# Where the weights of the values products and of attention's sums lie beside their moving data in SBUF

## The chip, the cores and the metric

The kernel runs on one core of a Trainium2 chip. The metric is the device time of one execution in microseconds (us), taken as the median of several runs. Every matmul here reads two operands from SBUF: 128 columns of weights, which are loaded into TensorE first, and the moving data, which are then streamed through it. The trace has a record for each of the two (PEld for the load, PE for the matmul), and it names the clock that TensorE was granted.

## The reference

Two groups of tokens (`x_prompt` and `x_sample`, each 512 x 1024 in float32) pass through the same trunk of two layers, and a final RMS norm closes it. Cut to what matters:

```python
def trunk(x, ...):
    # layer 0: differential attention, 8 heads, V is 512 x 2048
    h = rms_norm(x, norm_g[0], eps)
    q, k, v, gate = split(h @ da_w_in)            # da_w_in: 1024 x 8192
    q, k = rotary_half(q) * d ** -0.5, rotary_half(k)
    p = softmax(q @ k.T)                          # two maps per head
    a = p[:, :, 0] - lam * p[:, :, 1]
    o = rms_norm(a @ v, subln_g) * (1 - lambda_init) * silu(gate)
    x = x + o @ da_w_out                          # 2048 x 1024
    # layer 1: bidirectional retention, 8 heads, V is 512 x 2048
    h = rms_norm(x, norm_g[1], eps)
    q, k, v, gate = split(h @ ret_w_in)           # ret_w_in: 1024 x 6144
    o = retention(q, k, v, decay_fwd) + flipped retention(q, k, v, decay_bwd)
    o = rms_norm(o, subln_g) * silu(gate)
    x = x + o @ ret_w_out                         # 2048 x 1024
    return rms_norm(x, final_norm_g, eps)
```

## The kernel before

**Numbers in two parts.** All matmuls take `float32r` operands. To keep accuracy, each operand is split into a high and a low part (`hi_of` on ScalarE, `lo_of` on VectorE), and each product is the sum of three passes: high by high, high by low, low by high (`PASSES`).

**Four stages.** The input projection of layer 0 runs from about 40 to 640 us, attention with its output projection to about 1120 us, the input projection of layer 1 to about 1495 us, and retention with its output projection to the end. The input projections use a seven-product scheme in place of eight products per 2 x 2 block (`Unit`, products P1 to P7). The right operands of a projection, the `B` tiles made from the normed input, lie in `slot`s; the left ones are weights from HBM, combined on VectorE and split into the ring `ws` of seven buffers.

**Which operand is loaded and which moves.** In a "pair" unit (queries, keys, gates) the `ws` tile is loaded as TensorE's weights and a `B` tile of 512 columns moves (line 616). In a "wide" unit (the values V, eight units, four in each layer) it is the other way round: 128 columns of a `B` tile are loaded, and 256 columns of the `ws` tile move (line 626). One product of a wide unit is 4 token blocks x 4 parts of K x 3 passes = 48 matmuls, so the eight units have 8 x 7 x 48 = 2688. In attention, `av` (line 1198) forms the sum of values over keys: 128 columns of `vt` (V) are loaded, 256 columns of the transposed attention map `aT` move; 24 matmuls each for 32 pairs of token blocks, 768 in all. Retention has four kinds of 256-column matmuls: scores (line 1332, keys loaded, queries move), states (line 1356, `kt` loaded, V moves), the near part (line 1376, V loaded, scores move) and the far part (line 1384, state loaded, queries move). The output projections (line 908) load `oT` and move a `ws` tile of 512 columns; twelve of them, at the very end, move 256.

**Where the tiles lie.** The slots that matter lie in one tile called `arena`, 1024 words (4096 bytes) apart; `slot(..., shift)` moves a tile by so many words inside it. The other slots are tiles of 4096 bytes and begin at the same address modulo 256 as the arena (128). The seven `ws` buffers are separate tiles behind the arena, with small tiles (`pad`) between them, into which the kernel puts its small columns (norm sums, maxima, constants of up to 32 words). Every step from one 128-column or 256-column block to the next within a tile is a multiple of 256 bytes. So for each kind of matmul one number says how its two operands lie to each other: the distance from the start of the moving data to the start of the weights, modulo 256 bytes. "Distance" means this below. Before the change it follows from the shifts:

| matmuls | line | moving columns | count | weights at (bytes) | moving at (bytes) | distance |
|---|---|---|---|---|---|---|
| pair units | 616 | 512 | 3360 | 0 (`ws`) | 0 (`B`) | 0 |
| attention scores | 1133 | 512 | 384 | 0 | 0 | 0 |
| output projections | 908 | 512 (12 have 256) | 1542 | 0 | 0 | 0 |
| values products | 626 | 256 | 2688 | 0 (`B`) | -64 (`ws`) | 64 |
| attention's sums | 1198 | 256 | 768 | 64 (`vt`) | 0 (`aT`) | 64 |
| retention: scores | 1332 | 256 | 192 | 128 | 64 | 64 |
| retention: states | 1356 | 256 | 192 | 64 | 0 | 64 |
| retention: near part | 1376 | 256 | 384 | 0 | 64 | 192 |
| retention: far part | 1384 | 256 | 192 | 0 | 64 | 192 |

(Addresses are counted from the start of the arena, modulo 256.) Where one kind follows another, the next one's weights are loaded beside the last one's moving data, and the distance is that of these two: from a state (line 1356) to a score (line 1332) it is 128 - 0 = 128.

**Order of the work.** The whole program is recorded as a list of operations (`plan.op`) with modelled costs, then `Plan.arrange` orders it for each engine by those costs and by due times. Addresses have no part in the costs. SyncE's queue issues the DMAs.

Of the kernel before, what the change touches and what calls it, by code (L numbers as in the profile page):

```python
# [9 lines left out]
F32 = mybir.dt.float32  # L10
F32R = mybir.dt.float32r
# [4 lines left out]
P = 128  # L16
# [237 lines left out]
def trunk_kernel(  # L254
# [13 lines left out]
    ar = ctx.enter_context(tc.tile_pool(name="ar", bufs=1))  # L268
# [10 lines left out]
    def view(pool, tag, i, size, shape, dt=F32):  # L279


        n = math.prod(shape[1:])
        if (tag, i) not in places:
            if size <= 32 and pool in (cp, wk):
                k = next(k for k, used in enumerate(gaps) if used + size <= PAD - 16)
                places[tag, i] = pads[k][:, gaps[k]:gaps[k] + size]
                gaps[k] += size
            else:
                places[tag, i] = pool.tile([P, size], F32, tag=f"{tag}{i}", name=f"{tag}_{i}", bufs=1)
        t = places[tag, i][0:shape[0], 0:n]  # L290
        if dt != F32:
            t = t.bitcast(dt)
        if len(shape) == 3:
            t = t.rearrange("p (a b) -> p a b", a=shape[1])
        elif len(shape) == 4:
            t = t.rearrange("p (a b c) -> p a b c", a=shape[1], b=shape[2])
        return t

    def work(tag, shape, bufs, dt=F32, name=None):
        size = SIZE.get(tag, shape[1])  # L300
        return Buf(plan, tag, bufs, lambda i: view(wk, tag, i, size, shape, dt))

    PAD = 64
    gaps = [0] * (WS_BUFS - 1)
    arena = ar.tile([P, 18 * 1024 + 112], F32R, tag="arena", name="arena")
    rings, pads = [], []
    for i in range(WS_BUFS):
        rings.append(ar.tile([P, 1024 + 16], F32R, tag=f"ws{i}", name=f"ws_{i}"))
        if i < WS_BUFS - 1:
            pads.append(ar.tile([P, PAD - 16], F32, tag=f"pad{i}", name=f"pad_{i}"))  # L310

    def slot(n, shape, dt=F32R, shift=0):

        size = math.prod(shape[1:])
        at = None if n in (12, 13) or n >= 20 else n if n < 12 else n - 2
        if at is None:
            assert not shift
            cnt[0] += 1  # L320
            label = f"b_{cnt[0]}"
            return Buf(plan, f"b{n}", 1, lambda i: cp.tile(shape, dt, tag=f"b{n}", name=label))
        assert dt == F32R
        lo = at * 1024 + shift

        def make(i):
            t = arena[:, lo:lo + size]
            return t.rearrange("p (a b) -> p a b", a=shape[1]) if len(shape) == 3 else t
        b = Buf(plan, f"b{n}", 1, make)
        b.also = Buf(plan, f"edge{at + 1 if shift else at}", 1, None)  # L330
        return b

    def const(shape, tag, dt=F32, size=None):
        return Buf(plan, tag, 1, lambda i: view(cp, tag, i, size or math.prod(shape[1:]), shape, dt))

    def ws_t(shape, wide=False):


        def make(i):
            lo = 0 if wide else 16  # L340
            t = rings[i][:, lo:lo + 1024]
            if len(shape) == 3:
                return t.rearrange("p (a b) -> p a b", a=shape[1])
            return t.rearrange("p (a b c) -> p a b c", a=shape[1], b=shape[2])
        return Buf(plan, "ws", WS_BUFS, make)
# [24 lines left out]
    def bank(tag, name=None):  # L370
        return Buf(plan, tag, BUFS[tag], lambda i: view(pj if tag == "pj" else sc, tag, i, S, [P, S]))
# [38 lines left out]
    def dma(out, in_, r, w, kb, eng=None):  # L410

        q = eng or nc.sync
        plan.op("SP" if eng is None else "ACT", 0.62, lambda: q.dma_start(out(), in_()), r, w, lands=2.0 + kb / 200.0,
                kb=kb, load=any(isinstance(k[0] if isinstance(k, tuple) else k, Buf) for k in w))
# [436 lines left out]
    def load_v(src, i, shift):  # L851
        out = []
        for a in range(2):
            t = slot(i + a, [P, NT, 256], F32R, shift)
            dma(lambda a=a, t=t: t.t.bitcast(F32), lambda a=a: src[a].rearrange("p (t e) -> p t e", t=NT),
                [src], [t], 512)
            out.append(t)
        return out

    def load_sg(src):  # L860
        t = os_t(F32, "sg")
        dma(lambda: t.t, lambda: src[:], [src], [t], 512)
        return t
# [82 lines left out]
    v_d = {}  # L946
# [163 lines left out]
    qk, vt, sg, oT = {}, {}, {}, {}  # L1110
    st = [{} for _ in tiles]

    def fetch1(h, g, v=True):
        for j in range(2):
            for which in range(2):
                qk[h, g, j, which] = load_qk((qk_d[0, which, h, g], j), 6 * which + 2 * g + j, 0)
        if v:
            fetch1_v(h, g)

    def fetch1_v(h, g):  # L1120
        vt[h, g] = load_v(v_d[0, h, g], 10 + 4 * g, 16)
        sg[h, g] = load_sg(g_d[0, h, g])

    def scores(i):
# [115 lines left out]
    for i in range(N + 5):  # L1240
        if i % 2 and i > 2:
            fill(1, LAG)
            at(av, i - 3, N)
        at(scores, i, N)
        at(row_max, i, N)
        at(exps, i, N)
        at(combine, i, N)
        for n, when in enumerate((0, 1, 2, 3)):
            if i == when:
                step(proj, 1)  # L1250
                if n >= 2:
                    new_xN(n - 2, lambda t, n=n: (xs[n - 2][0, t * P:(t + 1) * P, :], []))
                if n == 3:
                    fetch1_v(0, 1)
        if not i % 2 or i < 3:
            fill(1, LAG)
        at(transp, i - 1, N)
        fill(1, LAG)
        if i % 2 == 0 and i > 3:
            at(weighed, i - 4, N)  # L1260
        if i < N and i % 4 == 2 and i > 4:
            nh, ng = tiles[i][0:2]
            if ng == 1 and nh + 1 < NH:
                fetch1(nh + 1, 0)
            elif ng == 0 and nh > 0:
                fetch1(nh, 1)
# [20 lines left out]
    qk, vt, sg, oT = {}, {}, {}, {}  # L1287
# [182 lines left out]
    for i in range(N2 + 1):  # L1470
        if i < N2:
# [9 lines left out]
            if i == N2 - 1:  # L1481
                for n in range(2):
                    f = fin_ps[n] = bank("sc", "fin")
# [67 lines left out]
```

## Time and profile before

| | |
|---|---|
| time, median of 3 runs | 1816.58 us (1816.56 to 1818.8) |
| the profiled execution | 1817.25 us, of which the span of the trace is 1815.2 us |
| TensorE (PE) busy | 1800.2 us, 99% of the span, 10299 matmuls |
| weight loads (PEld) busy | 1572.2 us, beside the matmuls |
| VectorE / ScalarE / GpSimd busy | 1477.1 / 895.2 / 171.6 us |
| granted TensorE clock | 0.999 |
| DMA | 328.81 MB, 181 GB/s on average |

A matmul's record is longer than the time by which it holds up the next one, since matmuls overlap. What one costs is the spacing: the time from its start to the start of the next. The timeline merges matmuls of one kind that follow each other; the start of the next row less the start of this row, over the count, is the mean spacing. Within a steady run the duration in the records follows the spacing at a constant difference, so that durations of single matmuls (minimum, median, maximum of a line) can be read as spacings too.

### The profile page before, as it was taken

The page shows a single profiled execution, that of the slowest core. Times are in us where ns is not written, and L with a number is a line of the kernel's source. Part 1 is how long each engine was busy: PE and PEld are TensorE (multiplying, and loading weights), DVE is VectorE, ACT ScalarE, POOL GpSimd, SP SyncE. Part 2 cuts the span into 40 slices and gives each one's busy share as a digit, 9 for nine tenths or more (in the row PEclk, how much of TensorE's full clock was granted, in tenths as well). Part 3 has the DMA queues.
Part 4 walks back from the last instruction along what each step waited for, and adds up shares of the span by engine and source line. Part 5 has one row for each costly group of instructions (what it writes and reads, how often), then busy time and mean ns, then how long its engine had stood idle before and what let it go on. Part 6 is the DMA issues. An engine that isn't in the chain of part 4 may idle for free.

```text
span 1815.2 us, 27774 instructions
## 1 busy us (share of the span) xinstructions
PE 1800.2 (99%) x10299; PEld 1572.2 (87%) x10299; DVE 1477.1 (81%) x2319; ACT 895.2 (49%) x1856; POOL 171.6 (9%) x323
## 2 busy tenths in 40 slices
PE   9999999999999999999999999999999999999998
PEld 6889889898988888888888888898989998888887
DVE  7967787778699888888888897877787967888887
ACT  7753344443333564555454866444444454443346
POOL 1000000000000023222322200000000000111113
PEclk9999999999999999999999999999999999999999
DMA  6444455654546694444454524465646459664652
GB/s 216 134 138 129 157 146 168 193 164 150 170 127 181 208 337 179 180 158 159 182 203 140 198 66 144 152 197 162 210 144 225 143 178 400 261 237 178 226 214 93
DMA packets 162767, 328.81 MB, mean 181 GB/s; under 512 B 12724, under 2 KB 76872, under 8 KB 162632
## 3 DMA queue, kind: packets, MB, share of 16 engines
q1 hardware_dynamic: 162304, 326.71, 53.3%
q8 instruction: 81, 1.33, 0.3%
q14 instruction: 54, 0.44, 0.1%
q10 hardware_dynamic: 328, 0.34, 0.1%
HBM read 209.55 MB, written 117.44 MB: 180 GB/s over the span
## 4 chain that ended last, share of the span: by engine, by line
PE 92%; DMA 2%; DVE 2%; ACT 2%; issue 1%; POOL 0%; SPq 0%; POOLq 0%; ACTq 0%; DVEq 0%
PE pj L616 20%; PE pj L908 18%; PE sc L616 10%; PE pj L626 10%; PE o L616 8%; PE o L1198 5%; PE sc L626 5%; PE sc L1133 4%; PE o L626 2%; PE o L1376 2%; PE tp L1178 1%; PE o L1384 1%; PE tp L1356 1%; PE sc L1332 1%; DMA raw<-in_ret_w_out_dram 1%
## 5 line engine op out<-in xcount | busy, mean ns | idle before, releaser
L908 PE MATMUL pj<-ws,arena 128*128 128x512 f32 x1542 | 390.0, 396 | 0.0
L908 PEld LDWEIGHTS pj<-ws,arena 128*128 128x128 f32 x1542 | 277.6, 188 | 51.1
L616 PE MATMUL pj<-b,ws 128*128 128x512 f32 x1080 | 263.1, 391 | 0.2 <-DVE e L661 0.2
L616 PEld LDWEIGHTS pj<-b,ws 128*128 128x128 f32 x1080 | 201.3, 188 | 41.6 <-DVE e L661 0.7
L420 DVE TENSOR_TENSOR ws<-st,ws 128x512 fp32r<-128x512 f32 (+1 forms) x192 | 148.8, 779 | 76.1 <-ACT ws L417 54.3
L913 DVE SCALAR_TENSOR_TENSOR b<-pj,pad,b 128x512 f32<-128x512 f32 (+1 forms) x257 | 190.6, 746 | 22.7 <-PE pj L908 21.5
L420 DVE TENSOR_TENSOR ws<-raw,ws 128x512 fp32r<-128x512 f32 (+1 forms) x164 | 142.0, 870 | 76.3 <-ACT ws L417 71.6
L417 ACT CAST ws<-st 128x512 fp32r<-128x512 f32 (+1 forms) x192 | 132.2, 692 | 127.3 <-PE pj L616 36.4
L616 PE MATMUL sc<-arena,ws 128*128 128x512 f32 x768 | 185.2, 390 | 0.0
L616 PE MATMUL o<-arena,ws 128*128 128x512 f32 x744 | 178.7, 391 | 1.1 <-ACT m L402 0.6
L616 PEld LDWEIGHTS sc<-arena,ws 128*128 128x128 f32 x768 | 144.0, 188 | 29.8
L417 ACT CAST ws<-raw 128x512 fp32r<-128x512 f32 (+1 forms) x164 | 125.8, 772 | 87.9 <-PE o L616 41.5
L616 PEld LDWEIGHTS o<-arena,ws 128*128 128x128 f32 x744 | 138.4, 188 | 30.5 <-DVE arena L480 1.4
L616 PE MATMUL pj<-arena,ws 128*128 128x512 f32 x648 | 158.9, 390 | 0.3 <-DVE arena L480 0.3
L616 PEld LDWEIGHTS pj<-arena,ws 128*128 128x128 f32 x648 | 120.8, 188 | 25.3 <-DVE arena L480 0.6
L1151 ACT ACTIVATE b<-sc,pad 128x512 f32<-128x512 f32 x128 | 87.8, 688 | 69.8 <-DVE pad L1141 68.8
L626 PE MATMUL pj<-ws,b 128*128 128x256 f32 x960 | 120.9, 281 | 0.0
L653 ACT COPY c<-pj 128x512 f32<-128x512 f32 x104 | 60.8, 586 | 120.5 <-PE pj L616 65.3
L626 PEld LDWEIGHTS pj<-ws,b 128*128 128x128 f32 x960 | 117.1, 189 | 0.6
L1133 PE MATMUL sc<-arena 128*128 128x512 f32 x384 | 99.9, 393 | 0.8 <-ACT b L1151 0.8
L1198 PEld LDWEIGHTS o<-arena 128*128 128x128 f32 x768 | 94.8, 189 | 3.1 <-ACT arena L417 0.7
L1198 PE MATMUL o<-arena 128*128 128x256 f32 x768 | 95.7, 281 | 0.5 <-ACT arena L417 0.5
(208 smaller groups left out, 2878.2 us busy)
## 6 DMA issues: line engine op xcount, KB each, us to landing
qk<-os SPq DMA_DIRECT2D x192, 256.0 KB, 3.6
arena<-qk SPq DMA_DIRECT2D x96, 512.0 KB, 5.5
raw<-in_da_w_in_dram SPq DMA_DIRECT2D x64, 512.0 KB, 4.9
v<-os SPq DMA_DIRECT2D x64, 512.0 KB, 3.9
arena<-v SPq DMA_DIRECT2D x64, 512.0 KB, 4.0
raw<-in_ret_w_in_dram SPq DMA_DIRECT2D x48, 512.0 KB, 4.8
os<-g SPq DMA_DIRECT2D x32, 512.0 KB, 7.8
g<-e SPq DMA_DIRECT2D x48, 256.0 KB, 4.7
```

What stands on the lines that cost most here:

```text
L417: act(n, lambda: nc.scalar.copy(dst(), src()), r, w)
L420: dve(n, lambda: nc.vector.tensor_tensor(dst(), src(), hi().bitcast(F32), op=ALU.subtract), r, w)
L616: nc.tensor.matmul(ps.t, a[u][0]()[:, k, :], bt[k][:, v, :], start=(opens and k == 0 and i == 0), stop=(k == 3 and i == 2), skip_group_che ...
L626: nc.tensor.matmul(ps[:, (t % 2) * 256:(t % 2) * 256 + 256], bt[k][:, v, t * P:(t + 1) * P], a[u][0]()[:, k, :], start=(opens and t % 2 == ...
L653: act(S, lambda c=c, ps=ps: nc.scalar.copy(c.t, ps.t), [ps], [c])
L908: nc.tensor.matmul(ps[:, here], o[a][:, e, t * P:(t + 1) * P], u[b][:, e, here], start=(m == 0), stop=(m == 5))
L913: axpy(n, lambda half=half, here=here, ps=ps: nc.vector.scalar_tensor_tensor(half, ps[:, here], rr[:, t % 2:t % 2 + 1], half, op0=ALU.mult ...
L1133: nc.tensor.matmul(s.t, q[:, a, t * P:(t + 1) * P], k[:, b, :], start=(n == 0), stop=(n == 2))
L1151: act(840, lambda j=j, s=s, m=m: nc.scalar.activation(p[:, j, :], s.t, AF.Exp, bias=m.t, accum_out=sm[:, 2 * j + n:2 * j + n + 1]), [s, m] ...
L1178: nc.tensor.transpose(tp[:, j * P:(j + 1) * P], p[:, 0, j * P:(j + 1) * P], ident.t)
L1198: nc.tensor.matmul(o[:, e * 256:(e + 1) * 256], v[b][:, j, e * P:(e + 1) * P], aT[a][:, j, :], start=(n == 0), stop=(n % 12 == 11), skip_g ...
L1376: nc.tensor.matmul(o[:, e * 256:(e + 1) * 256], v_[v][:, 2 * c + j, e * P:(e + 1) * P], a_[:, u, j * 256:(j + 1) * 256], start=(e == 0 and ...
```

## The change

Three sizes and two offsets change. The `ws` ring's buffers grow from 1040 to 1056 words, the small tiles between them shrink from 48 to 32 words (the distance from one ring buffer to the next stays 4352 bytes), and the arena's tail shrinks so that the ring begins at the same address modulo 256 as the arena. In a pair unit or an output projection the `ws` tile then begins at word 0 of its buffer instead of word 16, which is the same address modulo 256 as before: 0. In a wide unit it begins at word 28 instead of 0: 112 in place of -64. Attention's V (`vt`) is shifted by 36 words instead of 16: 144 bytes in place of 64. So the distance becomes 0 - 112 = 144 modulo 256 for the values products, and 144 - 0 = 144 for attention's sums. Nothing else changes its distance but transposes of tiles in the pool `wk`, which now begins 128 bytes earlier modulo 256: 192 transposes (lines 733 and 832) go from 0 to 128. The small columns are spread over six pad tiles in another way. Each engine has the same instructions in the same order as before.

```diff
@@ view
-                k = next(k for k, used in enumerate(gaps) if used + size <= PAD - 16)
+                k = next(k for k, used in enumerate(gaps) if used + size <= PAD - 32)
@@ trunk_kernel
-    arena = ar.tile([P, 18 * 1024 + 112], F32R, tag="arena", name="arena")
+    arena = ar.tile([P, 18 * 1024 + 64], F32R, tag="arena", name="arena")
...
-        rings.append(ar.tile([P, 1024 + 16], F32R, tag=f"ws{i}", name=f"ws_{i}"))
+        rings.append(ar.tile([P, 1024 + 32], F32R, tag=f"ws{i}", name=f"ws_{i}"))
...
-            pads.append(ar.tile([P, PAD - 16], F32, tag=f"pad{i}", name=f"pad_{i}"))
+            pads.append(ar.tile([P, PAD - 32], F32, tag=f"pad{i}", name=f"pad_{i}"))
@@ ws_t
-            lo = 0 if wide else 16
+            lo = 28 if wide else 0
@@ fetch1_v
-        vt[h, g] = load_v(v_d[0, h, g], 10 + 4 * g, 16)
+        vt[h, g] = load_v(v_d[0, h, g], 10 + 4 * g, 36)
```

## The prediction

> **What bounds the kernel now.** I read the page first, then who waited for whom on TensorE, then TensorE's groups with shapes kept apart, then the timeline around the lines that the change touches.
>
> ```profile
> span 1815.2 us, 27774 instructions
> PE 1800.2 (99%) x10299; PEld 1572.2 (87%) x10299; DVE 1477.1 (81%) x2319; ACT 895.2 (49%) x1856; POOL 171.6 (9%) x323
> PE 92%; DMA 2%; DVE 2%; ACT 2%; issue 1%; POOL 0%; SPq 0%; POOLq 0%; ACTq 0%; DVEq 0%
> ```
>
> ```profile
> PE sc L1027 <- DVE pad L428: 1.4, 1, 1.4
> PE tp L1045 <- DVE arena L480: 1.2, 2, 0.8
> PE o L1045 <- DVE b L404: 1.1, 1, 1.1
> PE sc L1133 <- ACT b L1151: 0.8, 1, 0.8
> PE sc L1332 <- DMA arena<-qk: 0.7, 1, 0.7
> ```
>
> TensorE is busy for 99% of the span, the chain that ended last runs through it for 92%, and its longest wait for any other engine is 1.4 us, at the start. So the time is the sum of the spacings of some ten thousand matmuls. The change removes none, adds none and reorders none: only where operands lie differs. What decides is the spacing of the matmuls with 256 moving columns.
>
> ```profile
> 162.45 5.82 PE L626 MATMUL o<-ws,arena 128*128 128x256 f32 x48
> 168.10 5.82 PE L626 MATMUL sc<-ws,arena 128*128 128x256 f32 x48
> 173.76 0.87 PE L626 MATMUL pj<-ws,b 128*128 128x256 f32 x6
> ...
> 600.69 2.88 PE L616 MATMUL pj<-b,ws 128*128 128x512 f32 x12
> 603.41 2.88 PE L616 MATMUL o<-arena,ws 128*128 128x512 f32 x12
> ```
>
> Two products of a wide unit take 173.76 - 162.45 = 11.31 us for 96 matmuls: a spacing of 117.8 ns. A product with 512 columns takes 603.41 - 600.69 = 2.72 us for 12: 226.7 ns. Twice the columns cost 108.9 ns more, so 256 columns alone account for at most 108.9 ns and about 9 ns of each spacing go somewhere else. Which part of that depends on the distance?
>
> ```profile
> L616 PE MATMUL sc<-arena,ws 128*128 128x512 f32 x768 | 185.2, 390 | 0.0
> L626 PE MATMUL pj<-ws,b 128*128 128x256 f32 x960 | 120.9, 281 | 0.0
> L1198 PE MATMUL o<-arena 128*128 128x256 f32 x768 | 95.7, 281 | 0.5 <-ACT arena L417 0.5
> L1376 PE MATMUL o<-arena 128*128 128x256 f32 x384 | 50.4, 280 | 0.0
> L1356 PE MATMUL tp<-arena 128*128 128x256 f32 x192 | 28.0, 282 | 0.0
> L832 PE MATMUL o<-ident,m 128*128 128x128 f32 x64 | 12.3, 273 | 0.0
> L908 PE MATMUL pj<-ws,arena 128*128 128x256 f32 x12 | 1.6, 283 | 0.0
> ```
>
> A record is longer than the spacing by a constant: 281 - 117.8 = 163 ns and 390 - 226.7 = 163 ns. So durations rank the distances: 283 ns (a spacing of 120) at distance 0 on line 908, 281 (118) at 64, 280 (117) at 192. Small differences, but 64 and 192 are both better than 0. For distance 128 there is one place: every sixth matmul of line 1356 is followed by a score.
>
> ```profile
> L1356 PE MATMUL tp<-arena x192: 275/281/286, 1502.2 to 1777.7; 128*128 128x256 f32 x192
> L626 PE MATMUL pj<-ws,b x960: 280/281/282, 173.8 to 1474.9; 128*128 128x256 f32 x192
> L626 PE MATMUL pj<-ws,arena x576: 275/281/367, 153.9 to 1455.2; 128*128 128x256 f32 x192
> L1198 PE MATMUL o<-arena x768: 275/281/383, 646.8 to 1016.9; 128*128 128x256 f32 x192
> ```
>
> (Minimum, median, maximum.) Five at 281 and one at 286 give the mean of 282 above, so I read 286 ns, a spacing of 122 to 123, as distance 128 in one transition. The minimum of 275 ns, a spacing of 112, says something else: at the same distance of 64 a faster pattern exists. The timeline shows where.
>
> ```profile
> 1172.33 1.58 PE L626 MATMUL pj<-ws,arena 128*128 128x256 f32 x12
> 1173.74 0.60 PE L733 MATMUL tp<-ident,e 128*128 128x128 f32 x4
> 1174.10 4.34 PE L626 MATMUL pj<-ws,arena 128*128 128x256 f32 x36
> 1178.28 2.90 PE L616 MATMUL pj<-b,ws 128*128 128x512 f32 x12
> 1181.02 1.22 PE L626 MATMUL o<-ws,arena 128*128 128x256 f32 x9
> ```
>
> Before the four transposes: 1.41 us for 12, or 117.5 ns. After them: 4.18 us for 36; the first is held up once (the maximum of 367 ns, a spacing of 204), and the other 35 take 3.98 us, or 113.6 ns each. The pattern lasts to the end of the run. So how the loading of the next weights falls beside the moving data is worth 4.2 ns a matmul with everything else equal, and a pattern once entered keeps itself up.
>
> **The change part by part.**
>
> *The 2688 values products and 768 sums of attention, distance 64 to 144.* No row shows 144. Bounds per matmul: below, the transposes, whose loads cost next to nothing (273 - 163 = 110 ns, so -8 ns); above, distance 128, the nearest row by bytes (+4.5 ns). Between them lies the fast pattern (-4.2 ns). I take the fast pattern: it is the only second level that these same instructions hold for dozens in a row, whereas 286 ns was seen in single transitions in which the moving tile changed as well. This is a choice between ends on either side of nothing, and the chances below say so. For 3456 matmuls less some 150 that are fast already (I found the run shown, three more like it in the second projection, and one in attention): 3306 x 4.2 = 13.9 us gained. A run entered without a gap needs a few matmuls to settle; with four in each of 56 + 32 = 88 runs, 352 x 4.2 = 1.5 us come back.
>
> The Trainium skill, "TensorE: Matmul & The Clock Gate", section "Back-to-back issue gap", gives N / 2.4 + 2.5 ns between warm matmuls, 109.2 ns for 256 columns. The rows lie 8.6 ns above it with weights loaded each time; if the new distance removed all of this, the gain would by that figure be 29.7 us.
>
> *The 512-column products behind them.* Their distance stays 0, but the pattern is carried over: behind the fast run above, 12 take 2.74 us where 12 elsewhere take 2.72. That is 0.02 us a run, 1.1 us for 56 runs. Attention's runs are followed by scores, where I find no such difference. What I can't bound from rows is a longer memory than that.
>
> *192 transposes, distance 0 to 128.* At the price of the 286 ns record, 192 x 5 ns = 1.0 us; their weight data come with half as much moving data, so I take 0 and keep 1.0 us for the range.
>
> *Writing and loading the moved tiles.* Tiles of the wide units now start 16 bytes past a multiple of 32, and so does `vt`.
>
> ```profile
> L420 DVE TENSOR_TENSOR ws<-raw,ws 128x1024 fp32r<-128x1024 f32 x56 | 68.5, 1222 | 49.6 <-ACT ws L417 45.4 <-PE pj L908 3.0 <-ACT os L417 1.1
> arena<-v SPq DMA_DIRECT2D x64, 512.0 KB, 4.0
> ```
>
> VectorE's largest writes into the ring come 56 times at 1222 ns, and before them it sat idle for 49.6 us in all; 10% more would be 6.8 us on an engine with that idle time, at which TensorE's longest wait is 1.4 us. Loads of `vt` land in 4.0 us and are issued two token blocks ahead, some 15 us of attention; twice as long would still be hidden. Cost 0. If the cover were gone: 32 loads of 4 us each, but no row suggests it. A gain for transfers into the pool that moved by 128 bytes would be hidden in the same way.
>
> *Small columns in other pads.* The same instructions in the same order; 0.
>
> Sum: -13.9 + 1.5 + 1.1 = -11.3 us. The profiled execution took 1817.25 us (span 1815.2 and 2.05 around it), 0.67 over the median of the three runs; so 1817.25 - 11.3 = 1806.0 for it, and 1805.3 as a median.
>
> **The rivals.**
>
> *Slower: 144 is a neighbour of 128.* The mechanism: loads and moving reads meet in the same part of SBUF over a window around 128 bytes, and 144 is only 16 bytes further. For it: the 286 ns row, and that 64 and 192, which lie farthest from 0 and 128, are the best rows. Against it: single transitions only. Its place is each run of lines 626 and 1198. On the straight line from 128 (+4.5) to 192 (-1) the price at 144 is +3.1 ns, 3456 x 3.1 = +10.7 us: 1827.3. With the full +4.5 it is 1832. It decides from a spacing of 118.9 ns up, which is +3.6 us or 0.2%.
>
> *Nothing happens.* Three distances within 3 ns (283, 281, 280) may mean that the distance hardly matters and the fast pattern is a matter of what ran before. Then the time stays at 1816.6. The Trainium skill, "SBUF — State Buffer", section "A bandwidth-pool intuition that's wrong (but worth ruling out)", gives TensorE a second, independent read port for weight loads, which by itself would leave no room for a distance to matter. Two spacings at one distance, and 120 against 118, bear that out only in part.
>
> *All of the loss goes.* With the transposes' 110 ns: 3456 x 8 = 27.6 us, 1789.
>
> **How the numbers follow.** I give the fast pattern 0.42 (1800 to 1811, at 1805 when all but the run-ins settle), the full removal 0.05, no change within 0.2% 0.13, and the neighbour of 128 0.40, of which about 0.08 lies above 1831. Within 0.2%, 3.6 us, is about what the measurement can't tell from no change. The range reaches from 1796, beyond the likeliest case, to 1831; out of it fall the full removal, the upper end of the neighbour and little else, some 0.16.
>
> **What would show it.** Right: medians of lines 626 and 1198 at 276 to 277 ns instead of 281, a timeline with 48 values products in 5.45 us instead of 5.65, and lines 1332 to 1384 as before. Line 616 should stay at 390 to 391 ns; if it rises, the pattern is carried over further than I took it, and at 3360 matmuls each nanosecond there costs 3.4 us, enough to turn the sign at 4. Wrong: medians of 284 ns or more (the neighbour of 128), or 281 (no effect). New waits of line 626 for VectorE or of line 1198 for a DMA would mean that the writes, not the reads, matter.

## The result and the profile after

The changed kernel takes 1808.47 us (median of 6 runs, 1807.72 to 1809.06) against 1816.57 us before (6 runs): a ratio of 0.9953 with a 95% interval of 0.994 to 0.9966, 8.1 us faster. The forecast was 1805 within 1796 to 1831, and faster.

The page of the changed kernel, first lines:

```profile
span 1806.5 us, 27774 instructions
PE 1792.9 (99%) x10299; PEld 1563.2 (87%) x10299; DVE 1476.6 (82%) x2319; ACT 895.0 (50%) x1856; POOL 172.0 (10%) x323
```

The span is 8.7 us shorter and TensorE is still busy for 99% of it. Its groups, as they were shown before:

```profile
L616 PE MATMUL sc<-arena,ws 128*128 128x512 f32 x768 | 185.2, 390 | 0.0
L626 PE MATMUL pj<-ws,b 128*128 128x256 f32 x960 | 116.9, 275 | 0.0
L1198 PE MATMUL o<-arena 128*128 128x256 f32 x768 | 97.1, 284 | 0.5 <-ACT arena L417 0.5
L1376 PE MATMUL o<-arena 128*128 128x256 f32 x384 | 50.4, 280 | 0.0
L1356 PE MATMUL tp<-arena 128*128 128x256 f32 x192 | 27.9, 281 | 0.0
```

The values products went from 281 to 275 ns (their four groups to between 275 and 277). Attention's sums, at the same new distance of 144, went the other way, from 281 to 284. The others stand where they stood. The minimum, median and maximum of two groups of values products and of the sums, with the first and last start of each:

```profile
L626 PE MATMUL pj<-ws,b x960: 275/275/282, 173.6 to 1466.4; 128*128 128x256 f32 x192
L626 PE MATMUL sc<-ws,arena x768: 275/275/275, 168.1 to 1452.7; 128*128 128x256 f32 x192
L1198 PE MATMUL o<-arena x768: 277/284/387, 641.2 to 1013.0; 128*128 128x256 f32 x192
```

All 768 matmuls of the second group took 275 ns: the spacing there no longer varies at all. The starts alone split the gain. Attention's sums now begin at 641.2 us instead of 646.8, so 5.6 us were gained before them. From their first to their last start it takes 371.8 us instead of 370.1: 1.7 us lost. From there to the last values product it takes 453.4 us instead of 458.0: 4.6 us gained in the second projection. Two products in the timeline:

```profile
162.63 5.64 PE L626 MATMUL o<-ws,arena 128*128 128x256 f32 x48
168.11 5.60 PE L626 MATMUL sc<-ws,arena 128*128 128x256 f32 x48
173.55 0.84 PE L626 MATMUL pj<-ws,b 128*128 128x256 f32 x6
...
680.12 3.03 PE L1198 MATMUL o<-arena 128*128 128x256 f32 x24
682.99 1.54 PE L1133 MATMUL sc<-arena 128*128 128x512 f32 x6
```

96 values products take 10.92 us, 113.8 ns each (117.8 before), the fast pattern of the prediction. 24 of attention's sums take 2.87 us, 119.6 ns each. Added up from the trace over all matmuls, from each start to the next:

| line | before, us | after, us | difference |
|---|---|---|---|
| 626, values products | 316.44 | 306.09 | -10.35 |
| 1198, attention's sums | 90.48 | 91.94 | +1.46 |
| 616, pair units | 768.38 | 768.81 | +0.43 |
| 908 and 1133 | 451.09 | 450.63 | -0.46 |
| 1332, 1356, 1376, 1384, retention | 113.15 | 113.10 | -0.05 |
| transposes of lines 733, 832 and 1178 | 39.87 | 39.85 | -0.02 |

These lines give -9.0 us; the few matmuls of lines 1027, 1045 and 1057 took 0.3 us more. In the fourth row 0.8 us less is line 1133, which before the change waited 0.8 us once for ScalarE and now does not. Little else moved. The longest waits, then VectorE's writes to the displaced ring and the loads of V:

```profile
PE sc L1027 <- DVE pad L428: 1.4, 1, 1.4
PE tp L1045 <- DVE arena L480: 1.2, 2, 0.8
PE o L1045 <- DVE b L404: 1.1, 1, 1.1
```

```profile
L420 DVE TENSOR_TENSOR ws<-raw,ws 128x1024 fp32r<-128x1024 f32 x56 | 68.3, 1220 | 47.0 <-ACT ws L417 42.9 <-PE pj L908 3.0 <-ACT os L417 1.1
```

```profile
arena<-v SPq DMA_DIRECT2D x64, 512.0 KB, 4.1
```

TensorE's longest waits are the same, VectorE's writes to the displaced ring take 1220 ns (1222), the loads of V land in 4.1 us (4.0).

### The profile page after: what moved, and what is told of

Its sections match the earlier page's. It is cut to its first block, busy times and chain, and to the rows that moved or that the text cites. A ratio compares the mean times of both kernels' runs of the same rounds, so it can differ in the third digit from the quotient of the medians.

```text
span 1806.5 us, 27774 instructions
## 1 busy us (share of the span) xinstructions
PE 1792.9 (99%) x10299; PEld 1563.2 (87%) x10299; DVE 1476.6 (82%) x2319; ACT 895.0 (50%) x1856; POOL 172.0 (10%) x323
## 4 chain that ended last, share of the span: by engine, by line
PE 92%; DVE 2%; ACT 2%; DMA 2%; issue 1%; POOL 0%; SPq 0%; POOLq 0%; ACTq 0%; DVEq 0%
PE pj L616 20%; PE pj L908 19%; PE sc L616 10%; PE pj L626 10%; PE o L616 8%; PE o L1198 5%; PE sc L626 5%; PE sc L1133 4%; PE o L626 2%; PE o L1376 2%; PE tp L1178 1%; PE o L1384 1%; PE tp L1356 1%; PE sc L1332 1%; DMA raw<-in_ret_w_out_dram 1%
## 5 line engine op out<-in xcount | busy, mean ns | idle before, releaser
L626 PE MATMUL pj<-ws,b 128*128 128x256 f32 x960 | 116.9, 275 | 0.0
L626 PEld LDWEIGHTS pj<-ws,b 128*128 128x128 f32 x960 | 113.2, 188 | 0.6
```

The source lines that it names most:

```text
L626: nc.tensor.matmul(ps[:, (t % 2) * 256:(t % 2) * 256 + 256], bt[k][:, v, t * P:(t + 1) * P], a[u][0]()[:, k, :], start=(opens and t % 2 == ...
```

## The experiments

The question was why one distance made one kind of matmul faster and another slower. Theory A: weights that begin 16 bytes past a multiple of 32 spoil the fast pattern (V begins so in the changed kernel, the `B` tiles do not). Theory B: the order of the three passes does. Each diff is against the changed kernel unless it says otherwise; durations are means of a group. From start to start in the traces the spacing is 161.7 ns less than the duration in runs that have settled on the fast spacing, and 163.6 less on line 626 before the change; so the step from 281 to 275 ns is one of 4 ns in spacing, not 6. Versions whose time has no range were run once; for those the durations are the evidence.

**values_only: attention's sums back at 64.**

```diff
-        vt[h, g] = load_v(v_d[0, h, g], 10 + 4 * g, 36)
+        vt[h, g] = load_v(v_d[0, h, g], 10 + 4 * g, 16)
```

> Only the values products keep the distance of 144; attention's V goes back to a shift of 16 words, a distance of 64. Theory (the two parts are separate and only the first gains): line 626 stays at a duration of 275 to 277 ns, line 1198 returns from 284 to 281 ns, and the time is 768 x 1.8 ns = 1.4 us below the changed kernel, near 1807.0. Rival (the pattern is carried from one kind of matmul to the next, so the two depend on each other): line 626 leaves 275 to 277 ns.

Measured: 1807.18 us (1806.37 to 1807.98), ratio 0.9948 (0.9935 to 0.996). Its groups:

```profile
L626 PE MATMUL pj<-ws,b 128*128 128x256 f32 x960 | 116.9, 275 | 0.0
L1198 PE MATMUL o<-arena 128*128 128x256 f32 x768 | 95.8, 281 | 0.5 <-ACT arena L417 0.5
```

The two parts are separate: line 626 keeps its 275 ns, line 1198 returns to 281. The time falls by 1.3 us; the intervals of the two ratios overlap, so for this small difference the durations are the evidence.

**sums_aligned: 144 for attention's sums with weights at a multiple of 64.**

```diff
-            qk[h, g, j, which] = load_qk((qk_d[0, which, h, g], j), 6 * which + 2 * g + j, 0)
+            qk[h, g, j, which] = load_qk((qk_d[0, which, h, g], j), 6 * which + 2 * g + j, 64 * which)
...
-        vt[h, g] = load_v(v_d[0, h, g], 10 + 4 * g, 36)
+        vt[h, g] = load_v(v_d[0, h, g], 10 + 4 * g, 64)
...
-            st[i]['aT'] = [slot(4 + u, [P, NT, 256]) for u in range(2)]
+            st[i]['aT'] = [slot(4 + u, [P, NT, 256], F32R, 28) for u in range(2)]
```

> Attention's sums keep the distance of 144, but now as in the values products: the weights begin at a multiple of 64 bytes (shift of 64 words) and the moving data lie 112 bytes past one (aT shifted by 28 words; the keys by 64 words, which is 0 modulo 256). Theory A (the start of the weights, 16 bytes past a multiple of 32, is what spoils attention's sums): line 1198 falls from 284 to 275 or 276 ns, 768 x 7 ns = 5 us, to about 1803. Theory B (the order of the three passes spoils them): line 1198 stays at 284 ns and the time at 1808.5.

Measured: 1804.35 us (1803.51 to 1805.75), ratio 0.9932 (0.9918 to 0.9945), the fastest version of the study. A group, its minimum, median and maximum, and a run in the timeline:

```profile
L1198 PE MATMUL o<-arena 128*128 128x256 f32 x768 | 93.7, 277 | 0.0
```

```profile
L1198 PE MATMUL o<-arena x768: 275/275/282, 640.9 to 1010.2; 128*128 128x256 f32 x192
```

```profile
672.31 2.93 PE L1198 MATMUL o<-arena 128*128 128x256 f32 x24
675.07 0.60 PE L1178 MATMUL tp<-ident,b 128*128 128x128 f32 x4
```

The same distance now gives a median of 275 ns. A run of 24 takes 2.76 us, 115.0 ns each, more than the 113.8 of a values product: it has to settle first. The spacings of single matmuls from one run of line 1198 in this trace, in ns, show it:

```
114 118 114 120 119 116 118 120 119 114 113 114 113 113 114 113 113 114 113 113 114 113 113 114
```

Nine matmuls wander (nine or eleven in 30 of the 32 runs), then the spacing stands still: starts are kept in whole nanoseconds, and 113, 113, 114 is how a constant 113.3 ns looks in them. The changed kernel's values products wander for nine as well (in 23 of their 28 runs) before they reach the same 113.3 ns. In the changed kernel the runs of attention's sums settle too, on 119 and 121 in turn.

**sums_order: the passes innermost, as in the values products.**

```diff
-                for a, b in PASSES:
-                    for j in range(NT):
+                for j in range(NT):
+                    for a, b in PASSES:
```

> Addresses as in the changed kernel; in attention's sums the loops over the token blocks and over the three passes are exchanged, so that the passes are innermost as in the values products. Theory B (the order of the passes): line 1198 falls from 284 to 275 or 276 ns, 5 us, to about 1803. Theory A (the start of the weights): it stays at 283 to 285 ns and the time at 1808.5.

Measured: 1810.03 us (1809.06 to 1811.16), ratio 0.9964 (0.9951 to 0.9976).

```profile
L1198 PE MATMUL o<-arena 128*128 128x256 f32 x768 | 97.4, 284 | 0.7 <-ACT arena L417 0.5 <-DVE arena L420 0.3
```

284 ns as before the exchange: theory B falls. (The time is 1.6 us above the changed kernel's, but the intervals overlap.)

**d160, d128: other distances for both.** The ring's wide tiles start at word 24 or 32, V is shifted by 40 or 32 words.

```diff
-            lo = 28 if wide else 0
+            lo = 24 if wide else 0
...
-        vt[h, g] = load_v(v_d[0, h, g], 10 + 4 * g, 36)
+        vt[h, g] = load_v(v_d[0, h, g], 10 + 4 * g, 40)
```

> Both distances 160 in place of 144: the ring's wide tiles start at word 24, attention's V is shifted by 40 words and so begins at a multiple of 32 but not of 64. If only the distance counts and 144 is a narrow good place, both lines go to 280 ns or more. If the good place is broad, line 626 stays at 275 to 277 ns. If a start at a multiple of 32 is enough for the weights, line 1198 comes under 281 ns.

> Both distances 128 in place of 144 (the ring's wide tiles start at word 32, attention's V is shifted by 32 words; weights at multiples of 64 bytes in both). The rival of the prediction took 128 for the bad place from single transitions with 286 ns, a spacing of 122 to 123. If it is bad in steady runs too, lines 626 and 1198 are both at 284 ns or more and the time is 3456 x 4 ns = 14 us or more above the kernel before, 1830. If the transitions cost that only because the moving tile changes, both lines stay between 280 and 283 ns.

Measured: 1826.46 us at 160 and 1825.13 us at 128. Line 626 from the arena and line 1198, first at 160, then at 128:

```profile
L626 PE MATMUL sc<-ws,arena 128*128 128x256 f32 x768 | 94.8, 282 | 0.0
L1198 PE MATMUL o<-arena 128*128 128x256 f32 x768 | 97.3, 282 | 0.5 <-ACT arena L417 0.5
```

```profile
L626 PE MATMUL sc<-ws,arena 128*128 128x256 f32 x768 | 94.8, 283 | 0.0
L1198 PE MATMUL o<-arena 128*128 128x256 f32 x768 | 97.1, 283 | 0.5 <-ACT arena L417 0.5
```

Both are 1 to 2 ns worse than 64. So the places to either side of 144, 16 bytes away, are bad ones; 144 is not on a slope between them. But the moving data begin at a multiple of 32 in both versions and not in the changed values products, so distance and start were changed together. The weights begin at a multiple of 32 in all four groups, and the sums at 160 stay above 281 ns: such a start alone is not enough. And 128 in steady runs costs half of what I had read from single transitions. The expectation of 284 ns there was a little too high.

**start32, start48: 144 for attention's sums with other starts.** V, `aT` and the keys are shifted by 40, 4 and 16 words (start32) or 44, 8 and 16 (start48), which also brings line 1133 to a distance of 192. The ring's wide tiles start at word 20 (distance 176) or 26 (152). The diff of start32:

```diff
-            lo = 28 if wide else 0
+            lo = 20 if wide else 0
...
-            qk[h, g, j, which] = load_qk((qk_d[0, which, h, g], j), 6 * which + 2 * g + j, 0)
+            qk[h, g, j, which] = load_qk((qk_d[0, which, h, g], j), 6 * which + 2 * g + j, 16 * which)
...
-        vt[h, g] = load_v(v_d[0, h, g], 10 + 4 * g, 36)
+        vt[h, g] = load_v(v_d[0, h, g], 10 + 4 * g, 40)
...
-            st[i]['aT'] = [slot(4 + u, [P, NT, 256]) for u in range(2)]
+            st[i]['aT'] = [slot(4 + u, [P, NT, 256], F32R, 4) for u in range(2)]
```

> Attention's sums keep the distance of 144 with weights that begin 32 bytes past a multiple of 64 (V shifted by 40 words, aT by 4, the keys by 16, so that line 1133 goes from a distance of 0 to 192). If a start at a multiple of 32 is enough, line 1198 is at 277 to 278 ns as with an aligned start; if it takes a multiple of 64, it stays at 283 to 285 ns. The values products go to a distance of 176 with aligned weights (word 20): at 160 they had 283 ns; if the good place is a narrow one at 144, line 626 is at 280 ns or more here too.

> Attention's sums at a distance of 144 with weights that begin 48 bytes past a multiple of 64 (V shifted by 44 words, aT by 8, the keys by 16). Theory A: 48 is no multiple of 32, so line 1198 is at 283 to 285 ns as with 16, while 0 and 32 gave 277 to 279. If instead only the start of 16 is bad, it stays at 277 to 279 ns. The values products go to 152 (word 26): 8 bytes beside the good place line 626 is at 275 to 277 ns if the good place is one of whole lines of 16 bytes that 144 only begins, at 280 ns or more if it takes 144 itself.

Measured: 1821.3 and 1850.25 us. First start32, then start48:

```profile
L1198 PE MATMUL o<-arena 128*128 128x256 f32 x768 | 93.0, 276 | 0.0
L626 PE MATMUL sc<-ws,arena 128*128 128x256 f32 x768 | 94.8, 282 | 0.0
```

```profile
L626 PE MATMUL sc<-ws,arena 128*128 128x256 f32 x768 | 102.4, 294 | 0.0
L1198 PE MATMUL o<-arena 128*128 128x256 f32 x768 | 96.1, 282 | 0.0
```

With weights at 32 past a multiple of 64 the sums are fast (276); at 48 they are not (282). That is the side theory A foretold, but not the size: I expected 283 to 285, and some runs settle at 117, others at 119 and 121. The values products are slow at 176, and at 152 they take 294 ns, a spacing of 129 to 131 (most runs settle at 122 and 138 in turn): 8 bytes beside the best place is the worst place seen.

**values_odd: the values products with weights as attention's V had them.**

```diff
-            t = slot(B_SLOT[name] + k, [P, 2, S])
+            t = slot(B_SLOT[name] + k, [P, 2, S], F32R, 4 * (B_SLOT[name] + k in {*range(20)} - {12, 13}))
...
-            lo = 28 if wide else 0
+            lo = 32 if wide else 4
```

> The values products keep the distance of 144, but against B tiles in the arena the weights now begin 16 bytes past a multiple of 32, as attention's V does in the changed kernel: those B tiles are shifted by 4 words, the ring's wide tiles to word 32 and its other tiles to word 4. B tiles outside the arena stay, so the values products against them go to a distance of 128, and pair units against them to 16. Theory A (weights must begin at a multiple of 32): line 626 from the arena (sc, o) goes from 275 to 283 or 284 ns, and from b it is at 282 to 283 ns, as at 128. Rival (attention's sums were spoilt by something of their own stage): line 626 from the arena stays at 275 or 276 ns.

Measured: 1841.69 us.

```profile
L626 PE MATMUL pj<-ws,b 128*128 128x256 f32 x960 | 121.7, 281 | 0.0
L626 PE MATMUL sc<-ws,arena 128*128 128x256 f32 x768 | 94.1, 283 | 0.0
L626 PE MATMUL o<-ws,arena 128*128 128x256 f32 x384 | 46.7, 281 | 0.0
L616 PE MATMUL sc<-arena,ws 128*128 128x512 f32 x768 | 189.3, 395 | 0.0
```

At the same distance of 144 the values products lose their gain too (283 and 281 against 275; the 281 is a little less than expected, as is the 281 from `b`): it is where the operands start, not the stage. The pair units rise from 390 to 395 ns, those against shifted `B` tiles included, although these keep a distance of 0.

**odd64: the old distance, with weights at 16 past a multiple of 32.** As start32, but `aT` and the keys are shifted by 20 and 32 words, V stays at the 36 of the changed kernel, and the ring's wide tiles start at word 12 (distance 208).

```diff
-            lo = 28 if wide else 0
+            lo = 12 if wide else 0
...
-            qk[h, g, j, which] = load_qk((qk_d[0, which, h, g], j), 6 * which + 2 * g + j, 0)
+            qk[h, g, j, which] = load_qk((qk_d[0, which, h, g], j), 6 * which + 2 * g + j, 32 * which)
...
-            st[i]['aT'] = [slot(4 + u, [P, NT, 256]) for u in range(2)]
+            st[i]['aT'] = [slot(4 + u, [P, NT, 256], F32R, 20) for u in range(2)]
```

> Attention's sums at the distance of the kernel before, 64, but with weights that begin 16 bytes past a multiple of 32 (V shifted by 36 words, aT by 20, the keys by 32, so that line 1133 is at a distance of 128). If such a start costs something at any distance, line 1198 is at 283 ns or more instead of 281. If it only keeps the fast pattern of 144 from settling, line 1198 stays at 281 ns. The values products go to 208 with aligned weights (word 12): if 144 is the only fast one of the multiples of 16 tried, line 626 is at 280 ns or more, as it was at 128, 160 and 176.

Measured: 1817.18 us.

```profile
L626 PE MATMUL sc<-ws,arena 128*128 128x256 f32 x768 | 93.5, 281 | 0.0
L1198 PE MATMUL o<-arena 128*128 128x256 f32 x768 | 93.0, 276 | 0.0
```

I expected 281 or more for the sums. They take 276: at the distance of the kernel before, with weights that begin just as theory A forbids, the pattern is fast. Theory A falls as I had put it. At a distance of 144 it could not be told from another reading: weights at a multiple of 32 mean moving data that begin 16 bytes past one. Sorted by that:

| matmuls | distance | moving data begin, modulo 32 | weights begin, modulo 32 | duration, ns |
|---|---|---|---|---|
| values, after | 144 | 16 | 0 | 275 |
| sums, sums_aligned | 144 | 16 | 0 | 277 |
| sums, start32 | 144 | 16 | 0 | 276 |
| sums, odd64 | 64 | 16 | 16 | 276 |
| values, start32 | 176 | 16 | 0 | 282 |
| values, odd64 | 208 | 16 | 0 | 281 |
| values and sums, before | 64 | 0 | 0 | 281 |
| sums, after | 144 | 0 | 16 | 284 |
| values (arena), values_odd | 144 | 0 | 16 | 281 to 283 |
| sums, start48 | 144 | 0 | 16 | 282 |
| values and sums, d128 | 128 | 0 | 0 | 283 |
| values and sums, d160 | 160 | 0 | 0 | 282 |

All four fast cases have moving data that begin 16 bytes past a multiple of 32, none of the groups at a multiple of 32 is fast as a whole, and the distance still decides among the former. (Retention's matmuls, which come in short runs, and the values products at 152 are not in the table.)

Single runs at a multiple of 32 can be fast all the same. Before the change, at 64, five of the 60 runs of lines 626 and 1198 reached about 113 ns and kept it to their end. Each stood right behind transposes, and its first matmul was held up (a spacing of 200 to 220 ns). A sixth run that began so, the first values product behind line 623, stayed at 117.7, and so did the run of sums behind line 832 in values_only, where their places are the old ones. So at 64 the fast spacing could be kept up from the old places too, but was seldom entered; with the places of odd64 all 32 runs entered it. That is a sorting of cases, not a mechanism.

**narrow16, narrow28: the 512-column products.** On top of sums_aligned, the ring's other tiles start at word 16 (line 616 at 64, line 908 at 192) or 28 (112 and 144).

```diff
-            lo = 28 if wide else 0
+            lo = 28 if wide else 16
```

> As the version with aligned sums, but the ring's tiles of pair units and of the output projections start at word 16: line 616 goes from a distance of 0 to 64, line 908 from 0 to 192. If the distance counts for 512 moving columns as for 256 (118 ns at 64 against 120 at 0), line 616 falls from 390 to 388 ns, 3360 x 2 ns = 6.7 us, and line 908 likewise, 3 us: 1795. If the loss of a 512-column product does not depend on it, both lines and the time stay as they are at 1804.

> As the version with aligned sums, but the ring's tiles all start at word 28: line 908 goes from a distance of 0 to 144 with aligned weights, line 616 to 112 with weights 48 bytes past a multiple of 64. If 144 with aligned weights is good for 512 moving columns as for 256 (6 ns below distance 0), the durations of line 908 fall from 397 to about 391 ns, 9 us in all. If weights that do not begin at a multiple of 64 always spoil it, line 616 stays at 390 ns or rises, by 3.4 us for each nanosecond.

Measured: 1825.98 and 1827.77 us against 1804.35. First narrow16, then narrow28:

```profile
L908 PE MATMUL pj<-ws,arena 128*128 128x512 f32 x1530 | 389.7, 398 | 0.0
L616 PE MATMUL sc<-arena,ws 128*128 128x512 f32 x768 | 190.1, 396 | 0.0
```

```profile
L908 PE MATMUL pj<-ws,arena 128*128 128x512 f32 x1530 | 390.6, 398 | 0.0
L616 PE MATMUL sc<-arena,ws 128*128 128x512 f32 x768 | 190.1, 394 | 0.0
```

With 512 moving columns a distance of 0 (390 ns on line 616) is the best seen. From start to start line 616 takes 788.8 us at 64 and 789.0 us at 112, against 769.5 in sums_aligned: 5.7 and 5.8 ns a matmul. (The durations put 112 lower, at 394 to 396 ns, because duration and spacing lie 1 ns closer together there.) Both my expectations of a gain missed: what is good for 256 columns does not carry over.

**both_good: the changed values products with the sums of start32.** As start32, with the ring's wide tiles at word 28.

```diff
-            lo = 20 if wide else 0
+            lo = 28 if wide else 0
```

> The values products as in the changed kernel, attention's sums at 144 with weights 32 bytes past a multiple of 64 (V shifted by 40 words, aT by 4, the keys by 16), which settled sooner: 114.2 against 115.3 ns of spacing with a multiple of 64. Line 626 at 275 to 277 ns, line 1198 at 277 to 278 ns; 736 x 1.1 = 0.8 us less than the version with aligned sums, less 0.3 us for the scores at 192: 1803.5 to 1804.5. If the version with aligned sums owed its time to something else than line 1198, it is at 1806 or more.

Measured: 1805.25 us (1804.82 to 1806.56), ratio 0.994 (0.9926 to 0.9953).

```profile
L908 PE MATMUL pj<-ws,arena 128*128 128x512 f32 x1530 | 389.5, 398 | 0.0
L1133 PE MATMUL sc<-arena 128*128 128x512 f32 x384 | 101.5, 396 | 0.3 <-ACT b L1151 0.3
L1198 PE MATMUL o<-arena 128*128 128x256 f32 x768 | 93.0, 276 | 0.0
```

The sums are the best of all, but the scores at 192 take 396 ns instead of the 393 of the kernel before, and the output projections, whose own distance did not change, 398 instead of 397. From start to start line 1198 takes 87.7 us against 88.5 in sums_aligned, but line 908 takes 361.7 against 360.7 and line 1133 90.0 against 89.6. So the median is 0.9 us above sums_aligned, not below it, and outside what I expected; the intervals overlap.

## Why the prediction was right, and where it failed

- *TensorE's spacing alone decides.* Right. The gain is in line 626; of the waits only one of 0.8 us, on line 1133, went away.
- *The values products go over to the fast pattern, -4.2 ns each.* Right, in kind and size: 117.8 to 113.8 ns in the timeline, 10.35 us over the line. The prediction's share for them was near 9.8. No row had shown 144, though, and the prediction called its choice one between ends. It noted that the tiles which move now begin 16 bytes past a multiple of 32, but only for what writes them; in the table above that start belongs to what makes a group fast. That the values products got it was luck.
- *Attention's sums do the same.* This is the step that failed. It held that one number, the distance, says how two operands lie to each other. The sums rose by 3 ns and cost 1.46 us where some 2.6 us of gain had been counted (746 matmuls at 4.2 ns, less 0.5 us for settling). With their tiles moved at the same distance (sums_aligned) they gained 2.0 us (90.5 to 88.5), and the time was 1804.35 us, against the forecast of 1805. With the changed kernel's places the forecast of -11.3 us became -8.7 in the profiled executions: 4.1 us were missing here, and the other lines came out 1.5 us better together. The time still fell within the range because the values products are 3.5 times as many as the sums.
- *Four matmuls to settle.* Mostly nine, in the values products as in sums_aligned's sums. For 24-matmul runs this matters: 277 ns on average with a median of 275. The values products come in 28 unbroken runs and not in 56, since most of their products follow each other; 28 x 9 = 252 matmuls to settle is close to the 56 x 4 = 224 of the forecast, so there the two errors nearly cancel.
- *A record is 163 ns longer than the spacing.* Nearly: by the starts 163.6 ns on line 626 before and 161.7 on the fast spacing. So the 275 ns read as 112 is 113.3. Line 1376, read as 117 at a distance of 192, has 117.7 from start to start, no better than 64.
- *512-column products carry 1.1 us over.* Small, as said: +0.43 us on line 616, which follows 24 such runs and not 56, and -0.46 on lines 908 and 1133. But in both_good line 908, whose own operands did not move, rose by 0.6 ns from start to start, so the caution about a longer memory was due. The 5 ns of line 616 in values_odd are another matter: its distance stayed, but both of its operands start 16 bytes later.
- *Transposes, writes, loads and small columns at nothing.* Right, by the rows above.
- *The rival "neighbour of 128".* Its premise was half right (128 is a slow place, 283 ns instead of the 286 read from single transitions), its step was wrong: 144 is no worse for lying beside it. A straight line between measured distances is no guide when the steps are 16 bytes.
- *The rival "nothing happens".* Excluded by 275 against 281 ns, and by 294 at 152. The Trainium skill, "SBUF — State Buffer", section "A bandwidth-pool intuition that's wrong (but worth ruling out)", gives weight loads an independent read port; taken to mean that placement does not matter, it disagrees with these rows, and the measurement decides: with the same instructions the duration went from 275 to 294 ns by where two tiles start.
- *The rival "all of the loss goes".* The lowest spacing on which runs settled in any version shown is 113.3 ns, where 110 would have been needed; the loss was about halved, not removed.

What stays open: why a start at 16 past a multiple of 32 and a distance of 64 or 144 let the pattern settle fast, and whether the values products would be fast at 64 with such a start; that wasn't tried. Nor were 128 and 160 tried with moving data 16 bytes past a multiple of 32.

## What to carry to other kernels

Where TensorE is busy for 99% of the span, compare the spacing of one and the same kind of matmul over the trace: two levels at equal shapes, as 118 and 113.6 ns here, suggest that there is something to gain without a change to the work. Placing the operands is worth trying then, both starts and not their difference alone, for each number of columns by itself, and on runs long enough to settle; the spacings of a single profiled run tell a nanosecond apart that the total time can't. The places tried at multiples of 16 bytes gave 275 to 284 ns and the one between them 294, and both neighbours of the good place were bad; so measure each place.

## What the runs showed of the hardware

- The spacing of 256-column float32r matmuls with new weights each time ranged from 113.3 ns (settled) to 129 to 131 ns by placement alone, at a granted clock of 0.998 to 1.0.
- In the versions where the placement is fast, a run wanders first (nine matmuls in most runs of the changed values products and of sums_aligned, seven or fewer in most of start32 and odd64) and then keeps a constant 113.3 ns. Other placements settle on spacings in turn (119 and 121; 122 and 138). Before the change the spacing on lines 626 and 1198 wandered between 116 and 120 ns throughout, except in five of the six runs behind transposes (about 113 ns).
- 512-column products are best at a distance of 0 (390 ns on line 616, against 394 to 397 at 64 and 112), where 256-column ones (283 ns for the twelve of line 908) are not. The distance alone does not decide there either: at 0 with both operands 16 bytes past a multiple of 32, line 616 took 395 ns (values_odd).
